# Differential attention on one core: from one score group a slot to two, in twenty slots

## The chip, the core and the metric

The kernel runs on one core of a Trainium2 chip. The metric is the device time of one execution in microseconds (us). A core has a matmul engine (TensorE; PE in the rows, with its weight loads as PEld), VectorE (DVE), ScalarE (ACT), GpSimd (POOL) and SyncE (SP), which run their own queues of instructions in order and wait for each other by semaphores. The compiled program fixes each queue's order.

## What is computed

One layer of differential attention, then one layer of a gated MLP, over 512 tokens of width 1024. The change touches the attention alone:

```python
def probs(qq, kk):
    s = jnp.einsum('bhqd,bhkd->bhqk', qq, kk).astype(jnp.float32) * scale + bias
    s = jnp.where(causal, s, -jnp.inf)
    return jax.nn.softmax(s, axis=-1)

a = probs(q_i[0], k1) - lam * probs(q_i[1], k2)
return jnp.einsum('bhqk,bhkd->bhqd', a.astype(v.dtype), v)
...
o = rms_norm(o, subln_g) * (1.0 - lam_init)
```

There are 16 heads, two softmax maps a head (each of depth 64), values of width 128, and four query blocks of 128 rows. Block i sees i + 1 blocks of keys.

## The kernel before

Attention runs in the stretch from 203 to about 508 us. Beside it the matmul engine computes the projections of the next pair of heads, and in the last pair the first part of the output projection. These are the filler: `project_qk` (line 491 on) yields after every three matmuls of 128x512 (lines 254 to 256), which is called a unit here, and a pair of heads takes 32 units. Its weights are split into a high and a low part as they arrive (`hi` on ACT, line 129; `lo` on DVE, line 130), and its finished accumulators `psqk` are copied out by ACT (line 504) and DVE (line 505).

The query blocks of a pair of heads are packed into five **groups** of up to 512 columns each: block 3 of the first head; its blocks 2 and 0; block 1 of both heads; block 3 of the second head; its blocks 2 and 0. A group goes through four steps:

- `scores` (line 694 on): six matmuls a block into two PSUM banks `pss`. DVE adds the bias and finds the row maximum (line 704), ACT takes the exponentials with their sums (line 707), and DVE inverts the sums and combines the two maps into `e` (lines 711 to 715).
- `flip` (line 721): four transposes of `e` into `pa`, which ACT copies to `at` (line 723).
- `values` (line 732): four 128x128 fp32 products into `po`, two machine matmuls each. After the last block of a head follows `normalise`: ACT squares `po` (line 662), DVE computes the inverse root in eleven small instructions (lines 180 to 192) and scales `po` into `on` (line 666).
- `close` (line 672): four transposes of `on` into `pto`, which DVE multiplies into `yT` (line 673).

A **slot** takes one group into `scores` and a group that is two slots older (LAG) through `flip` and `values`; its `todo` list puts scores at unit 0, the flip after unit 2, the values after unit 4 and a close after unit 5, of 6 or 7 units. There are 40 slots. All PSUM tiles share eight banks.

Of the kernel before, what the change touches and what calls it, by code (L numbers as in the profile page):

```python
# [10 lines left out]
F32 = mybir.dt.float32  # L11
# [5 lines left out]
P = 128  # L17
D = 1024
S = 512
BR = 2048  # L20
NH = 16
HALF = 64
NB = S // P
# [27 lines left out]
def build(ctx, tc, x, rel_bias, attn_norm, w_in, lq1, lk1, lq2, lk2, subln, w_out,  # L51
# [14 lines left out]
    def bank(name):  # L66
        return psum.tile([P, S], F32, tag="ps", name=name)
# [102 lines left out]
    make_identity(nc, ident)  # L170
    flip = const.tile([P, P], F32, name="flip")
    nc.vector.tensor_copy(flip, ident[:, ::-1])

    MAGIC = 1597463007.0 - 2.0 ** 22 - 2.0 ** 30
# [14 lines left out]
    def rsqrt(dst, ssum, n, scale):  # L189

        v = small.tile([P, n], F32, name=f"rv{n}")
        nc.vector.tensor_scalar(v, ssum, -0.5 * scale, -0.5 * EPS, ALU.mult, ALU.add)
        newton(dst, v, n)
# [56 lines left out]
    def proj_t(ps, w, c):  # L250

        cs = slice(c * P, (c + 1) * P)
        for k in range(KD):
            nc.tensor.matmul(ps, lhsT=w.hi[:, k, cs], rhs=hT[0][:, k, :], start=(k == 0), stop=False)  # L254
            nc.tensor.matmul(ps, lhsT=w.hi[:, k, cs], rhs=hT[1][:, k, :], start=False, stop=False)  # L255
            nc.tensor.matmul(ps, lhsT=w.lo[:, k, cs], rhs=hT[0][:, k, :], start=False, stop=(k == KD - 1))  # L256
            w.tick()
            yield
# [22 lines left out]
    def run(g):  # L281
        for _ in g:
            pass
# [126 lines left out]
    def residual(r, m, acc):  # L410
        def finish(b):
            ms = slice(m * S, (m + 1) * S)
            add = nc.vector.tensor_tensor(xr[:, b, ms], acc[b], xr[:, b, ms], ALU.add)
            square(r, b, m)
            if m == 0:
                half_mean(r, b)
            return add
        return finish
# [72 lines left out]
    def project_qk(p):  # L491
        qk = []
        for which in range(2):
            w = Chunk(qk_at[p] + which, 16)
            for j in range(2):
                ps = bank("psqk")
                yield from proj_t(ps, w, j)
                th = att.tile([P, NB, P], F32R, tag="qkh", name="qkh", bufs=8)
                tl = att.tile([P, NB, P], F32R, tag="qkl", name="qkl", bufs=8)
                sc = HALF ** -0.5 if which == 0 else 1.0  # L500
                pr = ps.rearrange("p (b n) -> p b n", b=NB)
                if which == 0:
                    pr = pr[:, :, ::-1]
                nc.scalar.activation(th, pr, AF.Copy, scale=sc)
                nc.vector.scalar_tensor_tensor(tl, pr, sc, th.bitcast(F32), ALU.mult, ALU.subtract)
                qk.append((th, tl))
        QK[p] = qk
# [123 lines left out]
    att = scope.__enter__()  # L631

    def fetch_values(g):
        V[g] = att.tile([P, 4, NB, P], F32, name="v")
        nc.gpsimd.dma_start(V[g].rearrange("p j b n -> p (j b n)"), vd[g])
# [8 lines left out]
    class Head:  # L644
# [12 lines left out]

        def normalise(self):
            ssq = small.tile([P, NB], F32, name="ssq")
            self.on = att.tile([P, NB, P], F32, name="on", bufs=2)  # L660
            for ii in range(NB):
                nc.scalar.activation(self.on[:, ii, :], self.po[:, ii * P:(ii + 1) * P], AF.Square,
                                     accum_out=ssq[:, ii:ii + 1])
            rs = small.tile([P, NB], F32, name="rso")
            rsqrt(rs, ssq, NB, 1.0 / P)
            nc.vector.tensor_tensor(self.on, self.po.rearrange("p (b n) -> p b n", b=NB),
                                    rs.unsqueeze(2).broadcast_to([P, NB, P]), ALU.mult)
# [7 lines left out]
    class Group:  # L675
# [10 lines left out]
        def scores(self):  # L686
            m = len(self.parts)
            ps = [bank("pss") for _ in range(2)]
            for hd, i, cs in self.parts:
                hd.need_bias()  # L690
                for t, (a, c) in enumerate(((0, 0), (0, 1), (1, 0))):
                    for f in range(2):
                        fs = slice(f * HALF, (f + 1) * HALF)
                        nc.tensor.matmul(ps[f][:, cs], lhsT=hd.q[a][fs, i],  # L694
                                         rhs=hd.k[c][fs, 0:i + 1].rearrange("p b n -> p (b n)"),
                                         start=(t == 0), stop=(t == 2))
            self.e = e = [att.tile([P, S], F32, name=f"e{f}", bufs=3 - f) for f in range(2)]
            nm = small.tile([P, 4], F32, name="nm")
            l = small.tile([P, 4], F32, name="l")
            for j, (hd, i, cs) in enumerate(self.parts):  # L700
                n = (i + 1) * P
                for f in range(2):
                    col = slice(2 * j + f, 2 * j + f + 1)
                    nc.vector.tensor_tensor_reduce(out=e[f][:, cs], in0=ps[f][:, cs], in1=hd.bias[:, S - n:S],  # L704
                                                   scale=-1.0, scalar=-NEG, op0=ALU.add, op1=ALU.min,
                                                   accum_out=nm[:, col])
                    nc.scalar.activation(e[f][:, cs], e[f][:, cs], AF.Exp, scale=-1.0, bias=nm[:, col],  # L707
                                         accum_out=l[:, col])
            r = small.tile([P, 4], F32, name="r")
            r2 = small.tile([P, 2], F32, name="r2")  # L710
            nc.vector.reciprocal(r[:, 0:2 * m], l[:, 0:2 * m])
            nc.vector.tensor_scalar(r2[:, 0:m], r[:, 1:2 * m:2], neglam, None, ALU.mult)
            for j, (hd, i, cs) in enumerate(self.parts):
                nc.vector.tensor_scalar(e[0][:, cs], e[0][:, cs], r[:, 2 * j:2 * j + 1], None, ALU.mult)
                nc.vector.scalar_tensor_tensor(e[0][:, cs], e[1][:, cs], r2[:, j:j + 1], e[0][:, cs],
                                               ALU.mult, ALU.add)

        def flip(self):
            pa = bank("pa")
            for c in range(0, self.width, P):  # L720
                nc.tensor.transpose(pa[:, c:c + P], self.e[0][:, c:c + P], ident)
            self.at = att.tile([P, S], F32, name="at", bufs=3)
            nc.scalar.copy(self.at[:, 0:self.width], pa[:, 0:self.width])  # L723

        def values(self):
# [16 lines left out]
    def out_units():  # L742
        for b in range(NB):
            acc[b] = bank(f"acc{b}")
        yield from out_half(i0, 0, hT_store, range(3), acc)

    PAIRS, VISITS, LAG = NH // 2, 5, 2
    line, heads = [], {}

    def visits(p):  # L750
        one, two = (Head(2 * p + i) for i in range(2))
        heads[p] = one, two
        return [Group((one, 3)), Group((one, 2), (one, 0)), Group((one, 1), (two, 1)), Group((two, 3)),
                Group((two, 2), (two, 0))]

    def slot(s, filler, units):

        todo = []
        if s < PAIRS * VISITS:
            if s % VISITS == 0:  # L760
                line.extend(visits(s // VISITS))
            todo.append((0, line[s].scores))
        if 0 <= s - LAG < len(line):
            todo.append((2, line[s - LAG].flip))
            todo.append((4, line[s - LAG].values))
        for i, ready in enumerate((2, 4)):
            p, r = divmod(s - LAG - ready - 1, VISITS)
            if r == 0 and 0 <= p < PAIRS:
                todo.append((5, heads[p][i].close))
        done = 0  # L770
        for at, f in todo:
            while done < min(at, units) and next(filler, StopIteration) is not StopIteration:
                done += 1
            f()
        while done < units and next(filler, StopIteration) is not StopIteration:
            done += 1

    tail = out_units()
    for p in range(PAIRS):
        if p % 2 == 0 and p < PAIRS - 2:  # L780
            fetch_values(p // 2 + 1)
        last = p == PAIRS - 1
        filler = tail if last else project_qk(p + 1)
        for r in range(VISITS + (LAG + 2 if last else 0)):
            slot(p * VISITS + r, filler, 6 + (r in (1, 3)))
        run(filler)
    scope.__exit__(None, None, None)
    quarters = tc.tile_pool(name="quarters", bufs=1)
    qp = quarters.__enter__()
# [120 lines left out]
    for n in range(BR // D):  # L910
        for i in range(7):
# [7 lines left out]
            units = product_n(ps, a, w, i in (0, 1, 3))  # L919
# [133 lines left out]
    last = residual(2, 1, acc)  # L1053
# [41 lines left out]
```

## Time and profile before

| what | value |
|---|---|
| time, median of 3 runs | 922.79 us (921.62 to 924.85) |
| time of the profiled execution | 921.33 us, of which the span shown in the profile is 919.6 us |
| mean granted clock of the matmul engine | 0.997 of full speed |
| matmul engine busy over the span | 898.9 us, 98% |
| DVE, ACT, POOL busy | 648.2, 476.2, 34.9 us |

The span runs from the first to the last instruction of one execution. Busy shares are averages over stages, and matmuls are pipelined: a row's duration overlaps the next row's, so the pace of the matmul engine is read from one start to the next.

### The profile page before, as it was taken

How to read it: one execution, taken by the hardware profiler on the slowest of the kernel's cores; microseconds unless marked ns; L12 is line 12 of the kernel's file. 1: busy time of each engine (PE TensorE's matmuls, PEld its weight loads, DVE VectorE, ACT ScalarE, POOL GpSimd, SP SyncE). 2: the span in 40 equal slices, each digit the busy share in tenths (PEclk: the TensorE clock that was granted, in tenths of full speed). 3: DMA queues.
4: the chain of work that ended last, by engine and by line, in shares of the span. 5: the costliest groups of instructions: out<-in, count | busy, mean ns of one | idle time of the engine just before them, and what ended most of it. 6: DMA issues, size and time to landing. Idle time of an engine off the chain costs nothing.

```text
span 919.6 us, 14089 instructions
## 1 busy us (share of the span) xinstructions
PE 898.9 (98%) x5393; PEld 765.2 (83%) x5393; DVE 648.2 (70%) x1399; ACT 476.2 (52%) x1015; POOL 34.9 (4%) x52
## 2 busy tenths in 40 slices
PE   7999999999999999999999999999999999999996
PEld 5878999987777777777778887688999999998885
DVE  6946675457878778777885939886796877676634
ACT  7625465455565556455754626665453535454532
POOL 0000100000000000000000002000100000000000
PEclk9999999999999999999999999999999999999998
DMA  8637755463224223321212704647555464534202
GB/s 296 217 99 214 193 183 116 149 195 104 58 69 128 79 71 103 100 62 58 70 48 90 275 0 115 180 109 216 119 179 119 157 138 138 116 116 155 85 13 91
DMA packets 55827, 115.47 MB, mean 126 GB/s; under 512 B 3965, under 2 KB 20398, under 8 KB 52432
## 3 DMA queue, kind: packets, MB, share of 16 engines
q1 hardware_dynamic: 49120, 79.70, 26.3%
q0 software_dynamic: 5584, 33.56, 15.4%
q10 hardware_dynamic: 1056, 1.32, 0.5%
q8 instruction: 42, 0.69, 0.3%
q14 instruction: 25, 0.20, 0.1%
HBM read 89.36 MB, written 6.33 MB: 104 GB/s over the span
## 4 chain that ended last, share of the span: by engine, by line
PE 82%; DVE 9%; ACT 5%; DMA 2%; issue 1%; ACTq 0%; DVEq 0%; POOLq 0%
PE px L319 15%; PE py L319 11%; PE psqk L254 5%; PE acc L273 5%; PE acc L275 5%; PE acc L274 5%; PE psqk L256 5%; PE psqk L255 5%; PE po L732 4%; PE psv L480 4%; PE pss L694 3%; ACT e L707 2%; PE px L307 2%; PE px L308 2%; PE px L309 2%; PE psy L980 2%
## 5 line engine op out<-in xcount | busy, mean ns | idle before, releaser
L374 DVE TENSOR_TENSOR lo<-quarter,hi 128x1024 fp32r<-128x1024 f32 x126 | 152.6, 1234 | 83.9 <-ACT hi L373 83.6
L373 ACT CAST hi<-quarter 128x1024 fp32r<-128x1024 f32 x126 | 128.9, 1047 | 122.7 <-DMA quarter<-quarter 45.7
L707 ACT ACTIVATE e<-e,nm 128x384 f32<-128x384 f32 (+3 forms) x128 | 70.7, 553 | 95.0 <-DVE nm L704 94.9
L130 DVE TENSOR_TENSOR lo<-raw,hi 128x512 fp32r<-128x512 f32 x144 | 94.2, 683 | 25.3 <-ACT hi L129 25.3
L254 PE MATMUL psqk<-hT,hi 128*128 128x512 f32 x256 | 110.3, 431 | 0.0
L129 ACT CAST hi<-raw 128x512 fp32r<-128x512 f32 x144 | 80.7, 619 | 40.9 <-DMA raw<-in_attn_w_in 13.8
L256 PE MATMUL psqk<-hT,lo 128*128 128x512 f32 x256 | 100.8, 394 | 0.0
L255 PE MATMUL psqk<-hT,hi 128*128 128x512 f32 x256 | 100.7, 393 | 0.0
L319 PE MATMUL py<-hT,hi 128*128 128x256 f32 x512 | 93.0, 283 | 0.0
L273 PE MATMUL acc<-hi,hT 128*128 128x512 f32 x224 | 89.2, 398 | 0.0
L274 PE MATMUL acc<-lo,hT 128*128 128x512 f32 x224 | 87.3, 390 | 0.0
L275 PE MATMUL acc<-hi,hT 128*128 128x512 f32 x224 | 87.3, 391 | 0.0
L319 PEld LDWEIGHTS py<-hT,hi 128*128 128x128 f32 x512 | 79.7, 192 | 0.0
L319 PE MATMUL py<-hT,lo 128*128 128x256 f32 x256 | 72.4, 283 | 0.0
L704 DVE CUSTOM_DVE_ANT_0 e<-pss,bias 128x384 f32<-128x384 f32 (+3 forms) x128 | 56.3, 485 | 10.5 <-PE pss L694 10.5
L254 PEld LDWEIGHTS psqk<-hT,hi 128*128 128x128 f32 x256 | 48.2, 188 | 13.3 <-issue 2.9
L256 PEld LDWEIGHTS psqk<-hT,lo 128*128 128x128 f32 x256 | 48.0, 188 | 10.7
L268 DVE TENSOR_TENSOR hT<-yT,hT 128x512 fp32r<-128x512 f32 x56 | 37.6, 688 | 25.6 <-PE acc L274 17.1
L255 PEld LDWEIGHTS psqk<-hT,hi 128*128 128x128 f32 x256 | 48.5, 189 | 6.1
L267 ACT CAST hT<-yT 128x512 fp32r<-128x512 f32 x56 | 33.5, 621 | 37.2 <-PE acc L274 28.6
L732 PEld LDWEIGHTS po<-v,at 128*128 128x128 f32 x320 | 38.9, 191 | 15.9 <-ACT at L723 15.6
L275 PEld LDWEIGHTS acc<-hi,hT 128*128 128x128 f32 x224 | 42.1, 188 | 9.0
(218 smaller groups left out, 2039.2 us busy)
## 6 DMA issues: line engine op xcount, KB each, us to landing
quarter<-in_sgu_w_in SPq DMA_DIRECT2D x48, 512.0 KB, 5.0
raw<-in_attn_w_in SPq DMA_DIRECT2D x38, 512.0 KB, 4.3
quarter<-quarter POOLq DMA_DIRECT2D x18, 1024.0 KB, 7.1
quarter<-in_attn_w_in SPq DMA_DIRECT2D x24, 512.0 KB, 4.7
raw<-in_attn_w_out SPq DMA_DIRECT2D x16, 512.0 KB, 4.4
raw<-in_sgu_w_out SPq DMA_DIRECT2D x16, 512.0 KB, 4.4
vd<-yT POOLq DMA_DIRECT2D x4, 1024.0 KB, 6.0
v<-vd POOLq DMA_DIRECT2D x4, 1024.0 KB, 5.2
```

The lines of the kernel that those rows point to most:

```text
L129: nc.scalar.copy(hi[:, sl], raw)
L130: nc.vector.tensor_tensor(lo[:, sl], raw, hi[:, sl].bitcast(F32), ALU.subtract)
L254: nc.tensor.matmul(ps, lhsT=w.hi[:, k, cs], rhs=hT[0][:, k, :], start=(k == 0), stop=False)
L255: nc.tensor.matmul(ps, lhsT=w.hi[:, k, cs], rhs=hT[1][:, k, :], start=False, stop=False)
L256: nc.tensor.matmul(ps, lhsT=w.lo[:, k, cs], rhs=hT[0][:, k, :], start=False, stop=(k == KD - 1))
L273: nc.tensor.matmul(acc[b], lhsT=yh[:, j, bs], rhs=w.hi[:, j, :], start=(k == 0), stop=False)
L274: nc.tensor.matmul(acc[b], lhsT=yh[:, j, bs], rhs=w.lo[:, j, :], start=False, stop=False)
L275: nc.tensor.matmul(acc[b], lhsT=yl[:, j, bs], rhs=w.hi[:, j, :], start=False, stop=(k == KB - 1))
L319: nc.tensor.matmul(ps[f // 2][:, f % 2 * H:(f % 2 + 1) * H], lhsT=w[x][:, k, f * P:(f + 1) * P], rhs=a[y][:, k, :], start=clear, stop=(k = ...
L373: nc.scalar.copy(hi[:, sl], raw[:, sl])
L374: nc.vector.tensor_tensor(lo[:, sl], raw[:, sl], hi[:, sl].bitcast(F32), ALU.subtract)
L707: nc.scalar.activation(e[f][:, cs], e[f][:, cs], AF.Exp, scale=-1.0, bias=nm[:, col], accum_out=l[:, col])
```

## The change

A slot now takes two groups (PER), so there are 20 slots with scores. All attention work of a slot stands in one visit with no unit between: the flips of the two groups of the slot before, a close where a head is due, the values of the two groups of two slots before, and the scores of two new groups. After the visit come the units. `want` sets how many: in proportion to the visits, but the projections of a pair must be done before its first group. In steady state the units after a visit are 20, 6, 13, 13 and 12, over and over, for two pairs of heads. The first map's buffers `e0` go from 3 to 4, `at` from 3 to 4, `on` from 2 to 1; `e1` keeps 2.

```diff
@@ class Head, normalise
-            self.on = att.tile([P, NB, P], F32, name="on", bufs=2)
+            self.on = att.tile([P, NB, P], F32, name="on", bufs=1)
@@ class Group, scores
-            self.e = e = [att.tile([P, S], F32, name=f"e{f}", bufs=3 - f) for f in range(2)]
+            self.e = e = [att.tile([P, S], F32, name=f"e{f}", bufs=4 - 2 * f) for f in range(2)]
@@ class Group, flip
-            self.at = att.tile([P, S], F32, name="at", bufs=3)
+            self.at = att.tile([P, S], F32, name="at", bufs=4)
@@
-    PAIRS, VISITS, LAG = NH // 2, 5, 2
+    PAIRS, VISITS, PER, LAG = NH // 2, 5, 2, 1
@@
-    def slot(s, filler, units):
-        todo = []
...
-            todo.append((0, line[s].scores))
-        if 0 <= s - LAG < len(line):
-            todo.append((2, line[s - LAG].flip))
-            todo.append((4, line[s - LAG].values))
...
-                todo.append((5, heads[p][i].close))
...
+    def slot(s):
+        of = lambda d: [g for g in range(PER * (s - d), PER * (s - d + 1)) if 0 <= g < PAIRS * VISITS]
...
+        for g in of(LAG):
+            line[g].flip()
+        for g in of(LAG + 2):
+            if g % VISITS in (2, 4):
+                heads[g // VISITS][g % VISITS // 2 - 1].close()
+        for g in of(LAG + 1):
+            line[g].values()
+        for g in of(0):
+            line[g].scores()
+
+    def filling():
+        for p in range(PAIRS - 1):
+            if p % 2 == 0 and p < PAIRS - 2:
+                fetch_values(p // 2 + 1)
+            yield from project_qk(p + 1)
+        yield from out_units()
...
+    filler, done = filling(), 0
+    for k in range(PAIRS * VISITS // PER + LAG + 3):
+        slot(k)
+        visit = PER * (k + 1)
+        want = max(32 * visit // VISITS, 32 * min(PAIRS - 1, (visit + PER - 1) // VISITS))
+        while done <= want and next(filler, StopIteration) is not StopIteration:
             done += 1
...
-        for r in range(VISITS + (LAG + 2 if last else 0)):
-            slot(p * VISITS + r, filler, 6 + (r in (1, 3)))
-        run(filler)
+    run(filler)
```

The order of the matmul engine before, at a place with scores of a 512-wide group (`pss`), between the values of one group (`po`) and the projections (`psqk`; L254 to L256 are one unit):

```order
L732 MATMUL po<-v,at 128x128 x4
L254 MATMUL psqk<-hT_103,hi 128x512
L255 MATMUL psqk<-hT_104,hi 128x512
L256 MATMUL psqk<-hT_103,lo 128x512
L254 MATMUL psqk<-hT_103,hi 128x512
L255 MATMUL psqk<-hT_104,hi 128x512
L256 MATMUL psqk<-hT_103,lo 128x512
L694 MATMUL pss<-qkh 128x512 x2
L694 MATMUL pss<-qkl,qkh 128x512 x2
L694 MATMUL pss<-qkh,qkl 128x512 x2
L254 MATMUL psqk<-hT_103,hi 128x512
```

Values and scores are two visits here with two units between them, and the flip comes two units after the scores.

The order of the matmul engine after the change, one whole visit in steady state (two flips `pa`, a close `pto`, two groups of values, then the scores of a 512-wide and the start of a 384 + 128-wide group):

```order
L721 MATMUL pa<-ident,e_3098 128x128 x4
L721 MATMUL pa<-ident,e_3134 128x128 x4
L672 MATMUL pto<-flip,on 128x128 x4
L732 MATMUL po<-v,at 128x128 x8
L694 MATMUL pss<-qkh 128x512 x2
L694 MATMUL pss<-qkl,qkh 128x512 x2
L694 MATMUL pss<-qkh,qkl 128x512 x2
L694 MATMUL pss<-qkh 128x384 x2
L694 MATMUL pss<-qkl,qkh 128x384 x2
L694 MATMUL pss<-qkh,qkl 128x384 x2
```

Nothing of the projections is left between them; 13 units stand ahead of this visit and 13 behind it.

The order of DVE after the change, in the visit ahead of that one, where a head ends (`ru` and `rso` are the last of the inverse root, `on` the scaled head, `e_3098` and `e_3099` the two maps of a new group):

```order
L186 TENSOR_TENSOR ru_3065<-ru_3065,ry_3064 128x4
L187 SCALAR_TENSOR_TENSOR rso<-ru_3065,ry_3064 128x4
L666 TENSOR_TENSOR on<-po,rso 128x512
L704 ISA e_3098,nm<-pss,bias 128x384
L704 ISA nm 128x1
L704 ISA e_3099,nm<-pss,bias 128x384
L704 ISA nm 128x1
L704 ISA e_3098,nm<-pss,bias 128x128
```

The normalisation of the finished head, which waits for that visit's values, now stands ahead of the reductions of the scores of the same visit; the flip of these scores is one slot later instead of two.

## Rows read from the trace of the kernel before

**Rows 1.** The page: the matmul engine's row, then a row of its group list

```profile
PE 898.9 (98%) x5393; PEld 765.2 (83%) x5393; DVE 648.2 (70%) x1399; ACT 476.2 (52%) x1015; POOL 34.9 (4%) x52
...
L130 DVE TENSOR_TENSOR lo<-raw,hi 128x512 fp32r<-128x512 f32 x144 | 94.2, 683 | 25.3 <-ACT hi L129 25.3
```

**Rows 2.** Busy time by stretch: one pair of heads, 308.45 to 345.03 us

```profile
core 0: us, PE busy (x) PEld busy (x) DVE busy (x) ACT busy (x) POOL busy (x), PEclk, DMA share, GB/s
...
308.45:345.03 36.58, 36.16 (x213) 28.08 (x213) 27.94 (x97) 20.24 (x66) 1.07 (x2) 1.00 0.25 73
```

**Rows 3.** Waits from 202 to 510 us: total us, times, longest

```profile
PEld po L732 <- ACT at L723: 15.6, 37, 1.1
...
PE po L732 <- ACT at L723: 3.2, 7, 0.7
```

**Rows 4.** Timeline of PE, 257 to 266 us: start, us, instruction

```profile
257.06 0.40 PE L256 MATMUL psqk<-hT,lo 128*128 128x512 f32 x1
257.38 0.50 PE L694 MATMUL pss<-qkh 64*128 64x512 f32 x2
...
258.27 0.50 PE L254 MATMUL psqk<-hT,hi 128*128 128x512 f32 x1
258.61 0.39 PE L255 MATMUL psqk<-hT,hi 128*128 128x512 f32 x1
258.84 0.40 PE L256 MATMUL psqk<-hT,lo 128*128 128x512 f32 x1
...
259.77 0.60 PE L721 MATMUL pa<-ident,e 128*128 128x128 f32 x4
260.12 0.47 PE L254 MATMUL psqk<-hT,hi 128*128 128x512 f32 x1
260.44 0.40 PE L255 MATMUL psqk<-hT,hi 128*128 128x512 f32 x1
...
261.70 1.16 PE L732 MATMUL po<-v,at 128*128 128x128 f32 x8
262.61 0.48 PE L254 MATMUL psqk<-hT,hi 128*128 128x512 f32 x1
...
264.86 0.45 PE L694 MATMUL pss<-qkh 64*128 64x384 f32 x2
...
265.87 0.50 PE L254 MATMUL psqk<-hT,hi 128*128 128x512 f32 x1
```

**Rows 5.** Timeline of PE in a later stage, 560.91 to 561.71 us

```profile
560.91 1.03 PE L827 MATMUL ptx<-ident,yT 128*128 128x128 f32 x8
561.71 0.48 PE L273 MATMUL acc<-hi,yh 128*128 128x512 f32 x1
```

**Rows 6.** Timeline of PE at 462 us, where no projection stands between

```profile
462.25 0.60 PE L672 MATMUL pto<-flip,on 128*128 128x128 f32 x4
462.78 0.44 PE L694 MATMUL pss<-qkh 64*128 64x384 f32 x2
```

**Rows 7.** Chain that ended last, 284 to 291 us: start, us, what

```profile
284.46 1.15 ACT on L662 x8
...
287.81 0.69 DVE on L666
...
288.50 0.33 DVE e L704
...
291.48 0.60 PE po L732 x3
```

**Rows 8.** Timeline of DVE, 262 to 270 us: brackets hold the idle time

```profile
262.05 0.75 DVE L715 SCALAR_TENSOR_TENSOR e<-e,r,e 128x512 f32<-128x512 f32 x1
...
265.97 0.56 DVE L704 CUSTOM_DVE_ANT_0 e<-pss,bias 128x384 f32<-128x384 f32 x1 [1.06 <-PE pss L694]
...
268.90 0.18 DVE L711 RECIPROCAL r<-l 128x4 f32<-128x4 f32 x1 [1.46 <-ACT e L707]
...
269.78 0.88 DVE L715 SCALAR_TENSOR_TENSOR e<-e,r,e 128x384 f32<-128x384 f32 x2
```

More of the change, by code (lines that the diff above doesn't have):

```diff
@@ L754, in visits @@
                 Group((two, 2), (two, 0))]
-    def slot(s, filler, units):
-        todo = []
-        if s < PAIRS * VISITS:
-            if s % VISITS == 0:
-                line.extend(visits(s // VISITS))
-            todo.append((0, line[s].scores))
-        if 0 <= s - LAG < len(line):
-            todo.append((2, line[s - LAG].flip))
-            todo.append((4, line[s - LAG].values))
-        for i, ready in enumerate((2, 4)):
-            p, r = divmod(s - LAG - ready - 1, VISITS)
-            if r == 0 and 0 <= p < PAIRS:
-                todo.append((5, heads[p][i].close))
[L770 to L775, printed above, removed]
-            done += 1
[L778 to L783, printed above, removed]
-        for r in range(VISITS + (LAG + 2 if last else 0)):
-            slot(p * VISITS + r, filler, 6 + (r in (1, 3)))
-        run(filler)
+    def slot(s):
+        of = lambda d: [g for g in range(PER * (s - d), PER * (s - d + 1)) if 0 <= g < PAIRS * VISITS]
+        for g in of(0):
+            if g % VISITS == 0:
+                line.extend(visits(g // VISITS))
+        for g in of(LAG):
[5 more added lines that the diff above has]
+            line[g].values()
+        for g in of(0):
+            line[g].scores()
[11 more added lines that the diff above has]
+        while done <= want and next(filler, StopIteration) is not StopIteration:
+            done += 1
+    run(filler)
     scope.__exit__(None, None, None)
```

## Prediction

> **What bounds the kernel now.** I read the page first: the matmul engine is busy 98% of the span [rows 1]. An average over stages says little about this change, so I cut out one pair of heads in the middle of attention. [...] So the matmul engine sets this stage, idle for only 0.42 us a pair, and VectorE is second at 76%. The list of waits says where the idle time lies: the value products wait for ScalarE's copy of the transposed scores, 3.2 us in all at the matmuls and 15.6 us at their weight loads, which run ahead [rows 3]. The timeline then shows what the busy time is made of, from start to start: the reader is to see how a visit to attention slows its neighbours.
>
> **What a visit costs on the matmul engine** [rows 4]. In steady projection one 128x512 matmul follows another after 0.23 us (258.61 to 258.84).
> Scores: from the last projection ahead (257.06) to the third behind (258.84) are 1.78 us. Three of those starts belong to projections, 0.69 us, so the visit costs 1.09. Its six half-height matmuls run as three pairs over 512 columns; at the same pace they need 0.69. The edges therefore cost 0.40 us: late entry, a slow first pair, a late exit, a slow first projection.
> Flip: four transposes take 0.35 us (259.77 to 260.12), and the projection behind takes 0.32 instead of 0.23: 0.44 with the edge.
> Values: 0.91 us (261.70 to 262.61) and the same edge of 0.09: 1.00.
> Close: four transposes, as the flip.
>
> **What the change does to these, for each slot of two groups.**
> Scores. Two visits become one, so one set of edges goes: 0.40 us.
> Flips. Apart, two cost 0.88. Eight transposes in a row were seen in a later stage and took 0.80 [rows 5], so the gain is 0.08, not a whole visit: 0.80 less 0.35 leaves 0.11 us for each further transpose, against 0.09 in a run of four.
> Values. Apart, two cost 2.00. Sixteen matmuls at 0.91 / 8 = 0.114 are 1.82: gain 0.18.
> Close. Behind other transposes four more cost 4 x 0.11 = 0.45, as much as apart: nothing.
> The step from values straight to scores does not stand in the trace. The nearest row is a close straight ahead of scores: 0.53 us to the scores [rows 6], where four transposes ahead of a projection take 0.35; that is 0.18 for the entry, against 0.09 from a projection. I take a loss of 0.09; the bounds are a gain of 0.09 (no entry cost at all) and a loss of 0.3.
> Sum: 0.40 + 0.08 + 0.18 - 0.09 = 0.57 us a slot, 11.4 over 20 slots.
>
> [...]
>
> Waits removed. The values now use a copy made a slot earlier, so the wait for it goes. Idle time of 0.42 us in each of eight pairs is 3.4 us; I take that. The bounds are 3.2 and, if every gap of the weight loads counted, 15.6; these gaps are mostly covered by the matmul ahead, so I go to 6 only.
>
> Moves that cost nothing, and their cover. One buffer fewer for `on`: the next head's squares must wait for the close, which stands ahead of the values in the same visit; without that cover it is 0.45 us a head. The deeper `e0` and `at` only hold groups for the next slot. Value and bias loads keep their number and nearly their order on POOL, and the raw weights theirs on SP; weights are split a chunk ahead, in the long gaps of 20 and 13 units.
>
> **What is late next.** Scores now have one gap of 4.2 us (6 units at 0.69) to 13.9 us (20 units) before their flip, where they had two slots. On their way lies VectorE.
> One group of two parts goes from its first reduction (265.97) to inverted sums in 2.93 us (268.90) and is scaled 1.76 later (269.78 + 0.88) [rows 8]. Two such groups in a row share ScalarE: 2.93 + 2.3 for the second's exponentials (the 2.93 without its first reduction and the inversion) + 1.76 = 7.0 us.
> Where a head ends, the normalisation stands ahead in the queues of ScalarE and VectorE. From the end of its values to the scaled head it takes 4.04 us (284.46 to 288.50) [rows 7]. That makes 11.0 us from the last value of the head to the second flip.
> The matmul engine meanwhile has half a run of values (0.9), scores (0.89 from 257.38 and 1.01 from 264.86 [rows 4], 0.2 for the entry), 13 units (9.0) and the first flip (0.4): 12.4 us. Slack 1.4. Two of the four visits with a normalisation begin with leftovers in VectorE's queue (splits of 0.68 us each [rows 1], copies of finished projections, the product of the close), which shift the chain by about 1 us: slack 0.4 with 13 units, and minus 0.3 with 12.
> The gap of 6 units has no normalisation ahead. There the second group is 512 wide: 2.93 + 1.5 + 1.6 = 6.0 us (estimates from the two-part group: two exponentials against four, three steps against five, the last of 0.75 at 262.05) from the first scored part; the matmul engine has the rest of the scores (1.3), 4.2 and the first flip (0.4), 5.9. With 0.4 for signals between the engines, 0.5 us late.
> So a wait of some 0.7 to 0.8 us, I take 0.7, in each of four cycles of five slots: 2.8 us. Bounds: 0, and 0.5 us a slot, 10 us.
>
> **Sum.** Against the profiled execution's 921.33 us: -11.4 - 3.4 + 2.8 = -12.0, which is 909.3. The median of the runs shown lies 1.5 above the profiled run, so I forecast 910.5 as a time to be measured, 1.3% faster.
>
> **The rivals.**
> 1. The new waits eat the gain. If each of the four normalising slots in a cycle is 0.7 us late, beside the short gap, that is 4 x (4 x 0.7 + 0.7) = 14 us against 14.8 gained: about 922, the same as before. For it: VectorE's 27.94 of 36.58 becomes about 80% of a shorter stretch, and it stands still while it waits for squares and exponentials. Against it: 11.0 us of chain lie under 12.4 of matmuls.
> 2. Slower. The place is the second flip of a visit: the whole matmul queue stands behind it. If the chain to it is more than 1.2 us a slot longer than I walked (leftovers of VectorE pile up from visit to visit, since the queue cannot overtake), 2 us of lateness in each of the 16 normalising slots costs 32 us less the 14.8 gained: about 940. It decides from 0.9 us a slot. Against it: the gap of 20 units in every cycle lets the queue catch up.
> [...]
> 3. A larger gain. All edges inside a visit vanish: two more of 0.09 a slot, no entry cost, no waits, and 6 us of old waits gone: 20 x 0.75 + 6 = 21, about 901.
>
> **How the numbers follow.** Forecast (about 903 to 918) 0.63; larger gain 0.11; partly eaten, still faster by over 0.3%, 0.04; eaten 0.09; slower 0.13. A difference of 0.3%, 2.8 us, is about what a measurement here can tell from none. Faster is 0.63 + 0.11 + 0.04 = 0.78, same 0.09, slower 0.13. The range runs from 901, the larger gain, to 922: only the scores' 8.0 and 3.4 of waits gained, 10 lost to new waits, is -1.4, or 921.4 against the median. It leaves out the slower case and a bit below.
>
> **What would show it.** One pair in mid-attention falls from 36.58 to about 35.1 us. The timeline shows one entry and one exit a visit, and from values to scores a step to price. Waits of the values for the copy go to nothing; in their place stand waits of flips for VectorE's last step at L715, after the gap of 6 units and that of 12 units, under a microsecond each. I am wrong if flips wait in every slot, if the step from values to scores costs over 0.5 us, or if the projections wait for a PSUM bank or for split weights, which I took as free.

## The result: 1.2% faster, and where it came from

The changed kernel takes 910.92 us (median of 4 runs, 909.98 to 913.83) against 922.24 us of the kernel before beside it: a ratio of 0.9877, with a 95% interval of 0.9861 to 0.9892. The profiled execution went from a span of 919.6 to 908.2 us. The forecast was 910.5. The sum came out, but its terms did not: the old wait was put 3.7 us too small, the edges with the new waits 1.3 us too large, and a loss of 3.1 us was not in it. That these offset each other is luck.

The page of the changed kernel, the matmul engine's row: it is still nearly always busy, so what has fallen is the busy time itself.

```profile
PE 885.3 (97%) x5393; PEld 774.6 (85%) x5393; DVE 645.3 (71%) x1399; ACT 476.9 (53%) x1015; POOL 34.4 (4%) x52
```

Next, busy time by stretch in the changed kernel: the stretch, its length, then busy time of each engine, granted clock, DMA share and rate. The first row, called attention from here on, runs from the first score product to the first transposes behind attention and holds the output projection too; the second is everything behind; the third is one full cycle of ten groups (five slots of two).

```profile
202.81:546.45 343.64, 340.71 (x1980) 287.09 (x1979) 263.76 (x845) 197.25 (x583) 9.49 (x17) 1.00 0.29 91
546.45:908.20 361.75, 347.74 (x2247) 315.15 (x2245) 257.98 (x371) 175.27 (x277) 14.55 (x15) 0.99 0.45 127
302.36:371.23 68.87, 68.46 (x429) 58.47 (x428) 54.54 (x192) 40.83 (x130) 2.68 (x5) 1.00 0.30 93
```

The same three stretches of the kernel before, between the same instructions:

```profile
202.89:560.91 358.02, 354.33 (x1979) 277.68 (x1979) 266.67 (x845) 195.93 (x583) 9.48 (x17) 1.00 0.28 87
560.91:919.60 358.69, 347.33 (x2247) 315.09 (x2245) 258.10 (x371) 175.92 (x277) 15.06 (x15) 0.99 0.46 129
308.45:381.62 73.17, 72.34 (x425) 56.15 (x424) 55.89 (x193) 40.47 (x131) 2.68 (x5) 1.00 0.29 87
```

Three readings. Attention is 14.38 us shorter, more than the whole gain. The part behind it, where nothing was edited, is 3.06 us longer. With 0.08 us before attention that is -14.38 + 3.06 - 0.08 = -11.40, the difference of the spans. And a cycle fell by 4.30 us, 3.88 of it busy time and 0.42 idle time; a cycle is two pairs, so a pair takes 34.4 us where [rows 2] have 36.58 and the forecast 35.1.

Waits of the matmul engine in the attention of the changed kernel: total, times, longest. The wait for the copy at L723 that [rows 3] show at the value products is gone; 1.7 us of waits at the flips have come.

```profile
PE pa L721 <- DVE e L715: 1.7, 3, 0.8
PE acc L273 <- DVE on L666: 0.5, 1, 0.5
PE pa L721 <- ACT at L723: 0.4, 1, 0.4
PE pto L672 <- DVE on L666: 0.2, 1, 0.2
```

A visit, in the timeline of the matmul engine (start, length, instruction), answers to [rows 4]:

```profile
298.04 0.39 PE L256 MATMUL psqk<-hT,lo 128*128 128x512 f32 x1
298.27 1.03 PE L721 MATMUL pa<-ident,e 128*128 128x128 f32 x8
299.14 0.60 PE L672 MATMUL pto<-flip,on 128*128 128x128 f32 x4
299.57 1.95 PE L732 MATMUL po<-v,at 128*128 128x128 f32 x16
301.45 0.44 PE L694 MATMUL pss<-qkh 64*128 64x384 f32 x2
```

From start to start: eight flips 0.87, a close 0.43, sixteen value products 1.88, and then the scores at once. The visit behind the gap of six units is the only one in a cycle that waits, 0.41 us ahead of its second flip:

```profile
307.43 0.60 PE L721 MATMUL pa<-ident,e 128*128 128x128 f32 x4
307.87 0.39 PE L732 MATMUL po<-v,at 128*128 128x128 f32 x2
308.67 0.63 PE L721 MATMUL pa<-ident,e 128*128 128x128 f32 x4 [0.41 <-DVE e L715]
```

The same moment on VectorE: the step that the flip waits for ends at 308.52.

```profile
307.77 0.75 DVE L715 SCALAR_TENSOR_TENSOR e<-e,r,e 128x512 f32<-128x512 f32 x1
```

Behind attention the waits have one line that differs. In the changed kernel:

```profile
PE px L307 <- ACT yT L897: 2.8, 3, 1.7
```

and in the kernel before:

```profile
PE px L307 <- ACT yT L896: 0.2, 1, 0.2
```

So there were two questions for the chip: what the 4.3 us of a cycle are made of (edges, the time that a change from one kind of matmul to another costs, as forecast; or the vanished wait for the copy, hidden in busy time), and what happened behind attention.

### The profile page after: what moved, and what is told of

Its sections match the earlier page's. It is cut to its first block, busy times and chain, and to the rows that moved or that the text cites. A ratio compares the mean times of both kernels' runs of the same rounds, so it can differ in the third digit from the quotient of the medians.

```text
span 908.2 us, 14110 instructions
## 1 busy us (share of the span) xinstructions
PE 885.3 (97%) x5393; PEld 774.6 (85%) x5393; DVE 645.3 (71%) x1399; ACT 476.9 (53%) x1015; POOL 34.4 (4%) x52
## 4 chain that ended last, share of the span: by engine, by line
PE 82%; DVE 10%; DMA 3%; ACT 3%; issue 1%; SPq 0%; ACTq 0%; DVEq 0%; POOLq 0%
PE px L319 15%; PE py L319 11%; PE psqk L254 6%; PE psqk L256 6%; PE psqk L255 6%; PE acc L273 5%; PE acc L275 5%; PE acc L274 5%; PE psv L480 5%; PE po L732 3%; PE pss L694 3%; DMA quarter<-quarter 2%; PE pa L721 2%; DVE lo L374 2%; PE psy L981 2%; PE px L307 1%
## 5 line engine op out<-in xcount | busy, mean ns | idle before, releaser
L254 PE MATMUL psqk<-hT,hi 128*128 128x512 f32 x256 | 101.7, 397 | 0.0
L256 PE MATMUL psqk<-hT,lo 128*128 128x512 f32 x256 | 99.9, 390 | 0.0
L255 PE MATMUL psqk<-hT,hi 128*128 128x512 f32 x256 | 99.9, 390 | 0.0
L254 PEld LDWEIGHTS psqk<-hT,hi 128*128 128x128 f32 x256 | 48.1, 188 | 12.9 <-issue 2.6
L256 PEld LDWEIGHTS psqk<-hT,lo 128*128 128x128 f32 x256 | 48.1, 188 | 10.1
L360 DVE TENSOR_TENSOR quarter<-quarter 128x1024 f32<-128x1024 f32 x36 | 43.3, 1222 | 11.5 <-DMA quarter<-in_sgu_w_in 10.8
```

## The experiments

The first score product starts anywhere from 202.2 to 205.2 us in the profiled executions of these kernels, which are alike up to there; so the times scatter by a few us. Small effects are therefore read from the period of ten groups in mid-attention. The first three columns of numbers are of the profiled execution, the time is the median of all executions, and the ratio is to executions of the kernel before made beside each kernel.

| kernel | ten groups, us | attention, us | behind it, us | time, us | ratio to before, 95% |
|---|---|---|---|---|---|
| before | 73.17 | 358.02 | 358.69 | 922.24 | |
| changed | 68.87 | 343.64 | 361.75 | 910.92 | 0.9861 to 0.9892 |
| even gaps | 68.27 | 343.47 | 362.4 | 912.55 | 0.9856 to 0.9906 |
| + unit in scores | 70.18 | 349.24 | 363.9 | 917.64 | 0.9925 to 0.9961 |
| + unit before scores | 68.44 | 343.67 | 366.8 | 911.23 | 0.9846 to 0.9902 |
| + unit in values | 68.47 | 342.07 | 361.9 | 909.93 | 0.9835 to 0.9878 |
| + unit in flips | 68.41 | 344.19 | 363.5 | 909.86 | 0.9849 to 0.9904 |
| before, values later | 71.48 | 350.95 | 360.39 | 916.65 | 0.9930 to 0.9963 |
| one group a slot | 71.26 | 350.97 | 363.3 | 918.62 | 0.9951 to 0.9975 |
| longer chain | 71.43 | 354.01 | 365.7 | 922.70 | 0.9993 to 1.0016 |
| changed, sum on VectorE | 68.88 | 343.68 | 358.68 | 906.55 | 0.9819 to 0.9846 |
| unit in values, sum on VectorE | 68.44 | 342.15 | 358.77 | 904.89 | 0.9804 to 0.9831 |
| before, sum on VectorE | 73.15 | 358.10 | 358.7 | 921.48 | 0.9983 to 1.0001 |
| before, buffers alone | 73.37 | 358.81 | 360.1 | 923.29 | 0.9998 to 1.0018 |

Part of the differences behind attention may lie in the granted clock. In the kernels with a unit in the scores or in the flips its mean over the profiled execution is 0.994, with a unit before the scores and with one group a slot 0.995, against 0.997 in the changed kernel. The longest wait for a px bank (the px banks hold products of the stage behind attention) is nearly the same, 1.8 us with a unit in the flips and with one group a slot and 1.74 in the changed kernel, where the clock from 624 to 634 us, around its end at 629.51, is 1.00. How much of the length is the clock's is not shown. The two longest parts, 366.8 and 365.7, also hold a wait of 2.8 and 2.1 us for L332, a copy of ScalarE out of a px bank, later on.

**Even gaps.** The share-out of the projection units alone.

```diff
-        want = max(32 * visit // VISITS, 32 * min(PAIRS - 1, (visit + PER - 1) // VISITS))
+        want = 64 * (k // VISITS) + (14, 32, 40, 52, 64)[k % VISITS]
```

> The changed kernel with the projection units shared out differently: gaps of 14, 18, 8, 12 and 12 units between slots where it has 12, 20, 6, 13 and 13. Theory A: the only waits left in the steady state are the 0.4 us a cycle behind the 6-unit gap, and the second flips behind 12 and 13 units have 0.75 to 1.7 us to spare, so the waits go and nothing takes their place: 1.6 us less than the changed kernel, about 909.3, and the second flip's wait for L715 gone. Rival B, the chain as the prediction walked it (slack 0.4 with 13 units, minus 0.3 with 12): two gaps lose a unit of 0.69 us each and wait 0.3 to 1.0 us, some 4 us more than is gained: about 913 to 915. This kernel is also the reference for the three with a unit put inside a visit.

```profile
301.24:369.51 68.27, 68.27 (x428) 58.41 (x428) 54.57 (x192) 40.81 (x130) 2.69 (x5) 1.00 0.29 93
```

Theory A on the steady state: no idle time is left in a cycle, 0.60 us less than the changed kernel, and the gaps of 12 units do not wait. The time did not follow: in the last pair the engine now waits 1.1 us at a flip and 1.8 us for a bank that L666 frees, and the part behind attention was 0.6 us longer. A miss on the time, by 3 us, which lies nearer to rival B's 913 to 915; the waits that B named are not in the cycle.

**One unit inside a visit**, at four places, all beside the even gaps. A unit is three projection matmuls; the gap behind has one fewer. The edit for the first place is shown; for the others the two added lines stand ahead of `scores` of the first group (from the third slot on), of `values` or of `flip` of the second.

```diff
+    def unit():
+        if next(filler, StopIteration) is not StopIteration:
+            done[0] += 1
...
         for g in of(0):
+            if g % PER:
+                unit()
             line[g].scores()
```

> The gaps of 14, 18, 8, 12 and 12 units, and one unit of three projection matmuls moved from each gap to a place between the scores of the slot's two groups. Theory A (edges): a second set of edges comes back, 0.40 us a slot, 20 slots: 8.0 us more than the kernel with the same gaps, about 917.3. Rival C (the gain lay in the waits for the copy, most of it hidden in the weight loads' 15.6 us): the scores cost the same however they stand, within 1 us of the kernel with the same gaps.

```profile
307.85:378.03 70.18, 70.18 (x425) 58.07 (x424) 54.69 (x193) 40.88 (x131) 2.70 (x5) 1.00 0.30 91
```

1.91 us a cycle, 0.38 a slot against 0.40 forecast, all of it busy time. The edges of the scores are real, and rival C is out for them. Attention as a whole is 5.8 us longer, not 8.0: its busy time rose by 7.4, and 1.6 us of the even gaps' waits, most of which are in the last pair, went.

> The gaps of 14, 18, 8, 12 and 12 units, one of each moved between the values and the scores of the visit, in 18 slots. As the prediction had the step (0.18 us from values to scores, against an exit of 0.09 and an entry of 0.09 when apart): no difference from the kernel with the same gaps. Theory A' (from the changed kernel's timeline, where 16 value products and the step take 1.88 us, 0.06 above 16 x 0.114): an exit of 0.09 and an entry of 0.09 in place of 0.06, 0.12 us a slot: 2.2 us more. Were the step dear (over 0.3), it would be some 2 us less.

```profile
302.28:370.72 68.44, 68.44 (x429) 57.65 (x428) 54.71 (x192) 40.79 (x130) 2.69 (x5) 1.00 0.31 93
```

0.17 us a cycle, 0.03 a slot, close to the prediction's "no difference": going straight from values to scores saves next to nothing, and costs nothing. The timeline shows why. Sixteen values take 1.70 us to the projection behind them:

```profile
298.79 1.95 PE L732 MATMUL po<-v,at 128*128 128x128 f32 x16
300.49 0.48 PE L254 MATMUL psqk<-hT,hi 128*128 128x512 f32 x1
300.81 0.39 PE L255 MATMUL psqk<-hT,hi 128*128 128x512 f32 x1
```

In the changed kernel they take 1.88 to the scores. The entry to the scores is thus 0.18, as the prediction had it; apart, an exit of 0.09 (300.49 to 300.81, less 0.23) and an entry of 0.09 come to the same.

> The gaps of 14, 18, 8, 12 and 12 units, one of each moved between the value products of the two groups. Theory A (edges): one more exit of 0.09 us a slot, 1.8 us more than the kernel with the same gaps. Rival C (no edges at the values, only their waits counted): no difference, within 0.5 us.

```profile
304.34:372.81 68.47, 68.47 (x430) 58.42 (x428) 54.40 (x192) 40.83 (x130) 2.69 (x5) 1.00 0.30 93
```

0.20 us a cycle, 0.04 a slot, where theory A wanted 0.09. Two runs of eight values with projections between them cost nearly as much as one of sixteen. (Attention is 1.4 us shorter than with the even gaps all the same: its waits in the last pair fell from 3.7 to 1.8 us.)

> Gaps of 14, 18, 8, 12 and 12 units, one unit of each moved between the flips of the slot's two groups. The kernel with those gaps takes 343.5 us from the first score product to the transposes behind attention, 339.8 of them busy. As the prediction had it (0.80 us for eight flips, 0.88 apart): 0.08 us a slot, 1.6 us more busy. Theory D (the changed kernel's timeline: eight flips take 0.87): nothing, within 0.4 us.

```profile
304.53:372.94 68.41, 68.41 (x428) 58.25 (x428) 54.52 (x192) 40.98 (x130) 2.69 (x5) 1.00 0.29 93
```

0.14 us a cycle, 0.03 a slot, nearer to nothing than to the 0.08 of the prediction. Over the whole of attention its busy time is 1.8 us above the even gaps, which looks like theory A's 1.6; but most of that lies elsewhere. Behind a wait of 1.75 us for L666 seven accumulations start 0.43 us apart in place of 0.23 (1.4 us in all), and the granted clock from 443 to 549 us is 0.98, against 1.00 from 440.5 to 546 us in the kernel with the even gaps, whose idle time there is 3.6 us (105.32 less 101.68). The period, taken at a clock of 1.00, is the cleaner number.

**Values one slot later, nothing merged.** The kernel before; the close moves one slot along with the values, and there is one slot more at the end (not shown).

```diff
-            todo.append((4, line[s - LAG].values))
+        if 0 <= s - LAG - 1 < len(line):
+            todo.append((4, line[s - LAG - 1].values))
```

> The kernel before with the values of a group one slot later than its flip, and the close with them; nothing merged. The stretch from the first score product to the transposes behind attention is 358.0 us before and 343.6 after. Theory A (as the prediction has it): only the idle time of 3.2 to 3.4 us at the value products goes, about 354.7, the time about 919. Theory D (from a kernel with a projection unit between two runs of eight values: a run there takes 0.81 us to the projection behind, where the kernel before has 0.91): the wait for the copy also lies inside the values' busy time, 0.10 us a visit, 40 visits: 4.0 us more, about 350.8, the time about 915.

```profile
304.88:376.36 71.48, 71.19 (x426) 57.13 (x425) 54.90 (x192) 40.12 (x131) 2.68 (x5) 1.00 0.29 89
```

The timeline of that kernel, eight values and the projection behind them, beside [rows 4]:

```profile
258.59 1.05 PE L732 MATMUL po<-v,at 128*128 128x128 f32 x8
259.40 0.48 PE L254 MATMUL psqk<-hT,hi 128*128 128x512 f32 x1
259.71 0.39 PE L255 MATMUL psqk<-hT,hi 128*128 128x512 f32 x1
```

Theory D, to 0.2 us: attention is 350.95 us long (the time, 916.65, is 1.7 above its 915). A run of eight takes 0.81 us where [rows 4] have 0.91 for the same instructions, and these two are typical: between 209 and 440 us, 28 of the 29 such runs that the timeline shows take 0.86 to 0.92 before, and all 25 take 0.80 or 0.81 here. Of the 1.69 us a cycle, 0.54 were idle time and 1.15 were counted as busy. The wait for the copy sat in the weight loads (15.6 us in [rows 3]) and stretched the products behind them. The loads of these two runs show it, before and with the values later:

```profile
261.69 0.97 PEld L732 LDWEIGHTS po<-v,at 128*128 128x128 f32 x8 [0.37 <-ACT at L723]
```

```profile
258.36 1.09 PEld L732 LDWEIGHTS po<-v,at 128*128 128x128 f32 x8
```

Before, they wait 0.37 us for the copy and begin 0.01 us ahead of the first product's start; with the values later they begin 0.23 us ahead of it.

**One group a slot.** Everything merged into one visit a slot, but no groups taken together.

```diff
-    PAIRS, VISITS, PER, LAG = NH // 2, 5, 2, 1
+    PAIRS, VISITS, PER, LAG = NH // 2, 5, 1, 2
```

> The changed kernel with one group a slot: 40 slots, each flip, close, values and scores in one visit, flips two slots behind their scores. Theory A (the prediction's edges of 0.09 behind flips and behind values go in every visit, 40 x 0.18 = 7.2, and 3.4 of waits): the stretch falls from 358.0 to about 347.4, the time to about 912, and pairing adds only some 4 us to that. Theory D (the merging of flips, values and scores is worth next to nothing, the values' wait for the copy 7.2, the pairing of scores 7.4 as measured): about 351 us, the time about 915, as with the values later alone.

```profile
308.55:379.81 71.26, 70.65 (x427) 58.58 (x426) 54.47 (x193) 40.79 (x131) 2.69 (x5) 1.00 0.29 89
```

Again theory D: 350.97 us, the same as with the values later alone (the time, 918.62, is 3.6 above its 915). In a cycle the merging takes 0.54 us off the busy time, and 0.32 come back as idle time, with waits of 0.6 us of the close for L666. Over the whole of attention the busy time falls by 1.6 us, where theory A had 7.2. From here to the changed kernel it is 2.39 us a cycle, 2.99 with the even gaps. The pairing of the scores is 1.91 of the 2.99 and the three other places come to 0.51; the remaining 0.57 match the idle time that goes, 0.61 a cycle here and none with the even gaps.

**A longer chain on VectorE**, in the changed kernel.

```diff
-            nc.vector.tensor_tensor(self.on, self.po.rearrange("p (b n) -> p b n", b=NB),
-                                    rs.unsqueeze(2).broadcast_to([P, NB, P]), ALU.mult)
+            for _ in range(4):
+                nc.vector.tensor_tensor(self.on, self.po.rearrange("p (b n) -> p b n", b=NB),
+                                        rs.unsqueeze(2).broadcast_to([P, NB, P]), ALU.mult)
```

> The changed kernel with VectorE's last step of the normalisation done four times over (the same numbers written again): 3 x 0.6, some 1.9 us more on the chain to the second flip at each of 16 heads. From the changed kernel's timeline the second flips have 1.7, 1.5 and 0.75 us to spare behind the gaps of 13, 13 and 12 units. Theory A (VectorE's chain decides from there): waits of about 0.2, 0.4 and 1.2 us in a cycle, 7 us in all, the time about 918. The chain as the prediction walked it (slack 1.4, 0.4 and minus 0.3): some 1.5 us in each of the 16, 24 us, about 935. Rival (the order of VectorE's queue lets other work wait in place of the flips): no more than 1 us, about 911.5.

```profile
PE pa L722 <- DVE e L716: 8.7, 10, 1.7
```

VectorE's busy time in attention rose by 27.6 us (291.32 less 263.76), 1.7 a head, and the flips then wait 8.7 us, 7.0 more than in the changed kernel, as theory A had it. The time, 922.70, is 4.7 above theory A's 918, and as slow as before: attention grew by 10.4 us, not 7 (3.0 are busy time: behind a wait of 1.74 us that ends at 454.69 twelve value products take 2.50 us to the scores, where sixteen take 1.88 in the changed kernel, and the mean granted clock of the execution is 0.993 against 0.997), and the part behind attention by 4.0. Still, attention is 4.0 us shorter than in the kernel before. So the prediction's first rival was within reach: with 1.7 us more on the chain at each head, most of what attention gained is gone.

**What happened behind attention.** Two weight sums run there as POOL transfers. The second, in the changed kernel (POOL's timeline, then SP's, then transfers with the time from issue to landing):

```profile
604.17 0.87 POOL L365 DMA_DIRECT2D quarter<-quarter  x1 [7.34 <-DVE lo L374]
```

```profile
604.03 0.88 SPq L355 DMA_DIRECT2D quarter<-in_sgu_w_in  x2
```

```profile
quarter<-in_sgu_w_in SPq DMA_DIRECT2D x2, 512.0 KB, 6.2
quarter<-quarter POOLq DMA_DIRECT2D x1, 1024.0 KB, 11.3
```

and in the kernel before:

```profile
617.98 0.87 POOL L365 DMA_DIRECT2D quarter<-quarter  x1 [6.70 <-DVE lo L374]
```

```profile
618.52 0.88 SPq L355 DMA_DIRECT2D quarter<-in_sgu_w_in  x2
```

```profile
quarter<-quarter POOLq DMA_DIRECT2D x1, 1024.0 KB, 8.5
quarter<-in_sgu_w_in SPq DMA_DIRECT2D x2, 512.0 KB, 9.2
```

Before, the sum is issued half a microsecond ahead of two loads and lands in 8.5 us, the loads in 9.2. After, it is issued 0.14 us behind them, and lands in 11.3, the loads in 6.2. ScalarE's queue stands at the split that needs the sum, with the copies that free the px banks behind it:

```profile
615.53 1.05 ACT L373 CAST hi<-quarter 128x1024 fp32r<-128x1024 f32 x1 [10.10 <-DMA quarter<-quarter]
...
618.05 1.06 ACT L897 COPY yT<-px 128x512 f32<-128x512 f32 x2
```

The test puts this one sum on VectorE, which waits there too.

```diff
+        def plus(self, n, dst, x):
+            for h in range(2):
+                sl = slice(2 * h, 2 * h + 2)
+                nc.vector.tensor_tensor(self.tiles[n, dst][:, sl], self.tiles[n, dst][:, sl],
+                                        self.tiles[n, x][:, sl], ALU.add)
...
             if i == 2:
-                self.add(n, "a", "d")
+                first = n == 1 and len(self.src) == 6
+                (self.plus if first else self.add)(n, "a", "d")
```

> The changed kernel with one sum of weights behind attention (a += d of the second column block) made by VectorE in two steps instead of a POOL transfer, which in the changed kernel lands 11.3 us after its issue, against 8.6 before, and holds ScalarE's queue so that px products wait 2.8 us for L897 against 0.2 before. Theory E (this late transfer takes back what attention gained beyond 11.4): the px waits go and the time falls by 2.5 us, to about 908.4, with the stretch from the first score product to the transposes behind attention as in the changed kernel, 343.6. Rival F (the transfer only shows what is late behind it: the next weights, or VectorE's own 2.4 us): the same 2 to 3 us of waiting for another releaser, time as the changed kernel, 910.9.

```profile
546.22:904.90 358.68, 347.23 (x2247) 315.05 (x2245) 260.71 (x373) 176.34 (x277) 13.31 (x14) 0.99 0.44 126
PE px L307 <- ACT yT L904: 0.3, 1, 0.3
```

The first line is the stretch behind attention, the second its wait. Theory E: the stretch is back at 358.68 us, what it is in the kernel before, and attention is untouched. The time fell by more than the 2.5 us expected: 4.4 by the medians, 3.3 by the spans of the profiled executions. Why the medians differ by more is open; in the four kernels named below the table, with the late sum and a lower mean clock, the part behind attention is 4.6 to 8.1 us longer than the 358.69 of the kernel before, not 3.1. With the kernel before as the control:

> The kernel before with the same sum on VectorE. Theory E: before the change that transfer held the px products for only 0.2 us, so the time stays within 0.5 us of 922.5. If it gains 2 us or more, the sum on VectorE is worth that of itself, and the changed kernel's gain from it proves nothing on the late transfer.

There it is worth little, if anything: 921.48 us, 1.0 below the 922.5 expected within 0.5, but 0.8 below the kernel before beside it, with an interval of 0.9983 to 1.0001; and the same 358.7 us behind attention. So the 3.06 us between the profiled executions are the late sum's. The two fixes together, this and a unit between the values beside the even gaps:

> The same sum on VectorE together with gaps of 14, 18, 8, 12 and 12 units and one unit between the values of the two groups, the kernel with the shortest stretch so far (342.1 us). Theory E: 1.5 us off the stretch and 2.5 off the waits behind it, 4 us less than the changed kernel, about 907. Rival F: only the 1.5, about 909.4.

904.89 us, 2 us under the expected 907, 1.8% under the kernel before and the fastest of these kernels; attention takes 342.15 us, behind it 358.77.

**Why does the sum land late?** The kernel before with the changed kernel's buffers and nothing else:

```diff
-            self.on = att.tile([P, NB, P], F32, name="on", bufs=2)
+            self.on = att.tile([P, NB, P], F32, name="on", bufs=1)
...
-            self.e = e = [att.tile([P, S], F32, name=f"e{f}", bufs=3 - f) for f in range(2)]
+            self.e = e = [att.tile([P, S], F32, name=f"e{f}", bufs=4 - 2 * f) for f in range(2)]
...
-            self.at = att.tile([P, S], F32, name="at", bufs=3)
+            self.at = att.tile([P, S], F32, name="at", bufs=4)
```

> The kernel before with the changed kernel's buffers alone: one for on, four and two for e, four for at. Theory as the prediction has it (the close stands ahead of what would wait): the period of ten groups stays 73.2 us and the time within 1 us of 922.4. If the normalisation has to wait for the close, up to 0.45 us a head, 7 us. Beside that it tells whether the tiles' new places make the sum behind attention land late: if so, the part behind attention is 361.7 us long as in the changed kernel, and the px products wait about 2.8 us for L896; if not, 358.7 and 0.2, as in the kernel before.

The buffers themselves cost about nothing (73.37 us for ten groups; a ratio of 0.9998 to 1.0018). The part behind attention is half-way, 360.1 us, with 1.3 us of px waits, and so it answers neither yes nor no. The first sum, some 8 us ahead, lands in 6.9 us before, 7.1 here, 7.6 in the changed kernel and all built on it, and 9.1 with the values later, which has the old buffers; so the buffers are not the whole cause. The second sum is issued 7.6, 7.7, 8.2 and 9.7 us after the first: the later the first lands, the later the second is issued. What sets the first sum's landing, and with it the order at the second, is open.

## Why the prediction was right, and which of its steps were not

- **Score edges, 0.40 a slot.** Right: 0.38. Of the edges only those of the half-height scores showed a price of this size; the further ones came to 0.03 to 0.04 a place. Twenty times 0.40 are the 8.0 in the prediction's range. What makes the price no run shows.
- **Flips 0.08, values 0.18, entry to the scores -0.09.** Putting a unit back cost 0.03 between the flips, 0.04 between the values and 0.03 between values and scores. The terms make 0.08, 0.09 (one of the values' two exits) and nothing (the other exit against the dear entry): 0.17 forecast, 0.10 found. Eight flips took 0.87, not the 0.80 of [rows 5]. The entry itself was right, 1.88 less 1.70. The values were not: in the step "values, apart, two cost 2.00" the 0.91 of [rows 4] held a hidden wait, and 0.91 / 8 carried it into the merged run too. Without it two cost 1.80 apart, and merged 1.70 and an exit of 0.09, so merging gains next to nothing. The slower projection behind a run of narrow products (0.32 us in [rows 4], in place of 0.23) is not an edge that merging removes; in the kernel with one group a slot all those places went, and attention stayed at 350.97 us.
- **The old wait, 3.4 us.** The step that failed most: "these gaps are mostly covered by the matmul ahead, so I go to 6 only". The 0.42 us a pair of the forecast are 36.58 less 36.16 in [rows 2]. With the values a slot later alone attention shrinks by 7.07 us, above that bound too. The missing 3.7 stood in no term: the wait was part of both sides of the values' sum, 2.00 and 1.82, and so dropped out of it.
- **New waits, 0.7 a cycle.** Right in kind and nearly in size: 0.41 behind the gap of six units, none behind that of twelve. There the slack was 0.75 us, not minus 0.3: the last L715 ends at 348.30 (347.42 + 0.88) and the second flip starts at 349.05 (348.61 + half of 0.87). In that visit VectorE's queue takes the last small steps of the normalisation between the reductions of the new scores, not ahead of them, and scales `on` only after three reductions (two of 512 columns, one of 384). That VectorE keeps the order of its queue, on which the second rival rests, the kernel before shows: a reduction starts at 288.42 us, behind `on` (287.81), though the last score products of its group end at 287.42. The 0.4 us for signals between the engines, behind the gap of six units, was the author's estimate and stands in no row; there the flip starts 0.15 us after the step that it waits for (308.52 to 308.67). Over all of attention the waits listed above come to 2.8 us, what the forecast had, but over half of that stands in the last pair and at the start. One sign of being wrong shows there, once: the output projection waits 0.5 us for L666.

```profile
340.01 0.69 DVE L704 CUSTOM_DVE_ANT_0 e<-pss,bias 128x512 f32<-128x512 f32 x1
340.63 0.08 DVE L704 DVE_READ_ACCUMULATOR2_ANT nm<- 128x1 f32 x1
340.63 0.16 DVE L186 TENSOR_TENSOR ru<-ru,ry 128x4 f32<-128x4 f32 x1
...
343.05 0.69 DVE L666 TENSOR_TENSOR on<-po,rso 128x512 f32<-128x512 f32 x1
...
347.42 0.88 DVE L715 SCALAR_TENSOR_TENSOR e<-e,r,e 128x384 f32<-128x384 f32 x2
```

- **Times 20 slots.** Too many. The gain holds from the first scores to those of the last pair, 14.84 us or three and a half cycles of 4.24; from there to the end of attention the changed kernel is 0.46 us slower than before (106.34 against 105.88).
- **"Moves that cost nothing".** True inside attention, as far as the buffers alone show it (73.37 us for ten groups against 73.17). Not foreseen: 3.06 us lost some 70 us behind attention, in a stage that the change does not touch.

By cycle the forecast was -2.85 for edges, -0.84 for old waits and +0.7 for new, -3.0; measured were -1.69 for the wait, -3.02 for merging and pairing and +0.41 for the new wait, -4.30.

For the whole the forecast was -3.4 for the old wait, -8.6 for edges and new waits together (-11.4 + 2.8), -12.0. Measured were -7.07 for the old wait, -7.31 for the rest of attention, +3.06 for the late sum and -0.08 ahead of attention, -11.40. So 3.7 too little, 1.3 too much and 3.06 not foreseen left a miss of 0.6 us in the sum: the mechanisms were right, with edges of the scores, a vanished wait and a new wait in their places, and the agreement of the total is luck. (The last step of the prediction's sum is off by 0.3 as well: 909.3 and 1.5 are 910.8, not 910.5.)

## What to carry to other kernels

A wait that the weight loads show is not free because the matmuls look busy: eight products behind a late copy took 0.91 us in place of 0.81, and moving the consumer one slot later, an edit of a few lines, was worth half of what attention gained. If a price is read from a row, see first whether the row holds a wait. Group first the work whose edges a run shows to be dear, here the half-height scores (0.38 us a slot), before the narrow products (0.03 to 0.04). And after a gain in one stage compare the length of the later stages too: here a transfer that landed 2.8 us later took back a fifth, and one sum moved to VectorE, which had idle time there, returned it.

## What the runs showed of the hardware that was not expected

- A projection unit between two runs of 128x128 products costs 0.03 to 0.04 us, between two visits of half-height scores 0.38.
- Behind a wait of the matmul engine of 1.75 us, with a unit in the flips, seven accumulations started 0.43 us apart in place of 0.23, and the granted clock from 443 to 549 us was 0.98. Around the changed kernel's wait of 1.74 us, from 624 to 634 us, it was 1.00.
- When a 1 MB sum on POOL's queue and two 0.5 MB loads on SP's are issued within 0.6 us of each other, the order goes with the landing time: with the sum ahead by 0.4 to 0.5 us it landed in 8.5 and 9.9 us and the loads in 9.2 and 9.1 (the kernel before, and that with the buffers alone); with the loads ahead by 0.12 to 0.16 us, in the changed kernel and the seven built on it that keep this sum on POOL, the sum took 11.2 to 11.5 and the loads 5.7 to 6.7. With the loads ahead by 1.6 us (the values later) it took 8.4. That the order is the cause is not shown: no run changes it alone.
